# Inverse behind the retention masks, merged softmax steps, a last half row in quarters, memory keys from 512-column products

## Chip, cores and metric

The kernel runs on one core of a Trainium2 chip. The metric is the device time of one execution in microseconds (us), lower is better. The compute engines are TensorE (PE in the rows; PEld is its weight load), VectorE (DVE), ScalarE (ACT) and GpSimd (POOL); SyncE (SP) issues most of the DMAs. Sums of matrix products land in PSUM, which is handed out here in banks of 512 fp32 columns.

## What is computed

A decoder trunk of two layers on 256 tokens of width 1024, with 256 memory tokens. Layer 0 mixes with RWKV-7 heads and retention heads side by side, layer 1 with differential attention; each layer then has a cross attention into the memory and a squared-ReLU MLP. The parts of the reference that matter here:

```python
# retention, by chunks of 128: scores under a decay mask (dmat is zero above the diagonal)
scores = einsum('bhncd,bhnmd->bhncm', qc, kc) * dmat
# RWKV-7: a recurrence over the tokens; the kernel solves it by chunks, with the inverse of a triangular matrix
state = state * w_t + (state @ a_t) * b_t + v_t * k_t
# differential attention, for each of 8 heads
p = softmax(logits)                       # two maps for each head
attn = p[:, :, 0] - lam * p[:, :, 1]
o = rms_norm(attn @ v, ln_w) * (1.0 - lam_init)
# cross attention: keys and values of the normed memory
mem_n = rms_norm(mem, mem_norm_w)
k, v = split(mem_n @ w_kv, 2)
# MLP and the end
h = h + square(relu(norm(h) @ w1)) @ w2
return rms_norm(h, final_norm_w)
```

## The kernel before

**Numbers.** Every large product is made in three products of fp32r operands: each operand is split into a high part (a rounded copy, by ScalarE) and a low part (the difference, by VectorE); `split` at line 128 writes both. A product is high x high, high x low and low x high, summed in PSUM (`mm3_w`, `mm3_x`). A weight piece of 128 x 1024 is loaded by SyncE and split by `wpiece` (line 138): one ScalarE instruction and one VectorE instruction for each of 262 pieces.

**Order.** The program is written stage by stage, but the order on each engine is made by a planner that takes, by priority and by its own model of the times, what is ready. An engine then runs its list strictly in that order. `urgent()` gives a very high priority, `high_priority()` (weight pieces) a high one, and `behind(a, b, ...)` adds an edge that only keeps the order of two instructions. Work without a near consumer, as the keys and values of the memory, fills TensorE where the chains of the RWKV part wait.

**Retention and inverse** (lines 578 to 666). The retention scores of four pairs of heads are small fp32 products into two banks shared by both halves `hq` (`ps1`) and further banks; VectorE multiplies them by the mask (lines 655, 657), ScalarE copies the rest (656). Then `inverse()` solves the triangular system by elimination: a loop of 31 steps of two dependent small VectorE operations (lines 595, 597), whose result `whole_inverse` uses later. All of it is independent of the masks.

**Memory keys** (`kv_chunk`, line 344). For each layer, eight blocks of 128 key columns, two by two in one bank: `proj_cols` runs 8 x 3 matmuls of 256 columns a block, and one ScalarE copy (layer 0, line 349) or one split (layer 1) takes both blocks out. Layer 1's four pairs are spread over the program: `kv1(1)` stands behind the output projection, behind the cross attention of layer 0, ahead of the differential attention, and behind it. `proj_wide` (line 312) is the form that the MLP's up projection uses: for each of 8 parts one matmul of 512 columns over the high and the low part of the activations, which lie side by side (`both`), and one of 256 columns with the low weights; the two halves of the bank are then added (lines 1036, 1037: a ScalarE copy `ul` and a VectorE sum).

**Differential attention** (`diff`, line 1087). The rows are normed, then transposed by TensorE (`turn(0)`, `turn(1)`) in the middle of the memory keys' blocks: behind block 0, and in the middle of block 1. `heads(hd)` makes the scores of a head for two row tiles `t` and two maps `c`, adds the bias, takes the maximum, the exponential with its sum, and then for each `t` a reciprocal (1133), a copy (1134), a factor (1136) and the weighted sum of the maps (1137). `turn_heads` transposes the result. `attend` needs the reciprocals again, squared (1180, 1181).

**End** (`mlp` with `on_sum`, `summed` at line 1218). Of the last of 16 chunks, the four half rows (t, hf) are finished one after the other: six matmuls of 512 columns, the sum into `h` (1063), then `summed`: ScalarE's square with its sum (1226), a step of the mean on VectorE (1232, 1234), GpSimd's power (1236); behind the last half row both tiles are scaled by ScalarE (left half) and VectorE (right half) and stored by SyncE (1244 to 1248).

## Time and profile before

| | us |
|---|---|
| median of 3 runs | 881.5 |
| lowest and highest | 880.51, 882.11 |
| the profiled execution, whole | 881.89 |
| its span, first to last instruction | 880.1 |

| engine | busy us | share |
|---|---|---|
| TensorE | 859.7 | 98% |
| VectorE | 590.4 | 67% |
| ScalarE | 455.2 | 52% |
| GpSimd | 30.8 | 3% |

The table is read from the top: an engine that is busy nearly all the time sets the span, except where it is held up. The ends of matmuls are modelled, and successive ones overlap, so the distance from one start to the next tells more of their cost than their length. Where an engine stood idle ahead of an instruction, the rows give the time in brackets with what released it.

### The profile page before, as it was taken

Reading aid. Unit: us, or ns where it says so; the run is one execution under the profiler, and the core shown is the slowest. Engines: PE = TensorE matmul, PEld = TensorE weight load, DVE = VectorE, ACT = ScalarE, POOL = GpSimd, SP = SyncE. Lnnn points to the kernel's source line nnn. Section 1 sums busy time; section 2 is a strip of 40 time slices with the busy share of each in tenths; the row PEclk is TensorE's granted clock in tenths of the full one; section 3 lists DMA queues with packets and bytes.
Section 4 is the critical chain, followed back from the end, with each engine's and each line's share of the span. In section 5 each row is a group of like instructions: output and inputs, shape, how many; then the busy total and the mean of one; then the engine's idle time right before and its main releaser. Section 6 shows DMA issues by size and latency. Waiting matters only on the chain.

```text
span 880.1 us, 14110 instructions
## 1 busy us (share of the span) xinstructions
PE 859.7 (98%) x5546; PEld 742.7 (84%) x5546; DVE 590.4 (67%) x935; ACT 455.2 (52%) x730; POOL 30.8 (3%) x51
## 2 busy tenths in 40 slices
PE   7999999999999999999999999999999999999996
PEld 5998789888899888888888898878998888888885
DVE  5679888574585576666666668776875766666665
ACT  5775444254564454444444546655655554444443
POOL 3000001010000000000000000000000000000001
PEclk9999999999999999999999999999999999999999
DMA  9754433135654646556555554434542466655551
GB/s 324 238 149 136 140 120 121 51 119 191 221 192 152 206 169 213 192 192 191 190 188 190 175 193 144 144 120 148 192 164 96 158 199 192 191 189 189 187 191 60
DMA packets 47078, 149.98 MB, mean 170 GB/s; under 512 B 4731, under 2 KB 4900, under 8 KB 46884
## 3 DMA queue, kind: packets, MB, share of 16 engines
q1 hardware_dynamic: 45456, 142.73, 50.0%
q10 hardware_dynamic: 1108, 3.72, 1.1%
q0 software_dynamic: 448, 2.63, 0.9%
q8 instruction: 43, 0.70, 0.3%
q14 instruction: 23, 0.19, 0.1%
HBM read 148.01 MB, written 2.63 MB: 171 GB/s over the span
## 4 chain that ended last, share of the span: by engine, by line
PE 90%; DVE 4%; ACT 2%; issue 2%; POOL 1%; DMA 1%; POOLq 0%; SPq 0%; DVEq 0%; ACTq 0%
PE acc L121 38%; PE mm L121 36%; PE tr L121 13%; DVE lo L129 1%; ACT hi L129 1%; PE tr L258 1%; DMA h<-in_x_dram 1%; PE tr L985 1%; PE acc L258 1%; POOL rs L230 0%; DVE xn L272 0%; ACT z L1130 0%; PE tr L1145 0%; PE tr L504 0%; POOL xn L1229 0%
## 5 line engine op out<-in xcount | busy, mean ns | idle before, releaser
L129 DVE TENSOR_TENSOR lo<-raw,hi 128x1024 fp32r<-128x1024 f32 x262 | 320.1, 1224 | 212.7 <-ACT hi L129 210.7
L129 ACT ACTIVATE hi<-raw 128x1024 fp32r<-128x1024 f32 x262 | 277.5, 1060 | 320.2 <-PE mm L121 111.5
L121 PE MATMUL mm<-xhl,hi 128*128 128x256 f32 (+1 forms) x784 | 189.1, 320 | 0.9 <-ACT xhl L129 0.7
L121 PEld LDWEIGHTS mm<-xhl,hi 128*128 128x128 f32 x784 | 129.4, 189 | 13.2 <-issue 2.0
L121 PE MATMUL mm<-xhl,lo 128*128 128x256 f32 x512 | 137.9, 282 | 0.0
L121 PE MATMUL acc<-hi,hl 128*128 128x512 f32 x256 | 100.2, 391 | 0.0
L121 PE MATMUL acc<-hi,hh 128*128 128x512 f32 x256 | 100.1, 391 | 0.0
L121 PE MATMUL acc<-lo,hh 128*128 128x512 f32 x256 | 99.7, 389 | 0.0
L121 PEld LDWEIGHTS mm<-xhl,lo 128*128 128x128 f32 x512 | 96.6, 189 | 2.5
L121 PE MATMUL tr<-xhl,hi 128*128 128x512 f32 x256 | 92.8, 395 | 0.0
L121 PE MATMUL acc<-hi,xhl 128*128 128x512 f32 x256 | 81.9, 396 | 0.0
L121 PE MATMUL tr<-xhl,lo 128*128 128x256 f32 x256 | 66.6, 281 | 0.0
L121 PEld LDWEIGHTS acc<-hi,hl 128*128 128x128 f32 x256 | 48.0, 188 | 11.2 <-DVE hl L129 0.9
L121 PEld LDWEIGHTS acc<-lo,hh 128*128 128x128 f32 x256 | 48.1, 188 | 10.5
L121 PEld LDWEIGHTS acc<-hi,xhl 128*128 128x128 f32 x256 | 47.7, 188 | 9.7
L121 PEld LDWEIGHTS acc<-hi,hh 128*128 128x128 f32 x256 | 48.1, 188 | 8.8
L121 PEld LDWEIGHTS tr<-xhl,hi 128*128 128x128 f32 x256 | 48.2, 188 | 8.5
L121 PEld LDWEIGHTS tr<-xhl,lo 128*128 128x128 f32 x256 | 48.2, 188 | 2.9
L121 PE MATMUL acc<-lo,xhl 128*128 128x512 f32 x128 | 50.4, 393 | 0.0
L121 PE MATMUL mm<-memh,hi 128*128 128x256 f32 x128 | 37.1, 290 | 0.0
L121 PE MATMUL mm<-meml,hi 128*128 128x256 f32 x128 | 37.1, 290 | 0.0
L121 PE MATMUL mm<-memh,lo 128*128 128x256 f32 x128 | 36.6, 286 | 0.0
(320 smaller groups left out, 1342.4 us busy)
## 6 DMA issues: line engine op xcount, KB each, us to landing
raw<-in_w_dram SPq DMA_DIRECT2D x64, 512.0 KB, 4.4
raw<-in_mlp_w_dram SPq DMA_DIRECT2D x64, 512.0 KB, 4.3
raw<-in_hyb_w_in_dram SPq DMA_DIRECT2D x16, 512.0 KB, 3.7
raw<-in_w_k_dram SPq DMA_DIRECT2D x16, 512.0 KB, 3.5
raw<-in_xattn_w_kv_dram SPq DMA_DIRECT2D x16, 512.0 KB, 3.8
raw<-in_w_q_dram SPq DMA_DIRECT2D x16, 512.0 KB, 4.1
raw<-in_xattn_w_o_dram SPq DMA_DIRECT2D x16, 512.0 KB, 3.5
raw<-in_w_dqk_dram SPq DMA_DIRECT2D x16, 512.0 KB, 3.5
```

Of the source, the lines that this page charges most:

```text
L121: ins = nc.tensor.matmul(o, lhsT=lhsT, rhs=rhs, start=start, stop=stop)
L129: return nc.scalar.activation(hi, src, AF.Copy), nc.vector.tensor_tensor(lo, src, r32(hi), op=ALU.subtract)
L258: nc.tensor.transpose(ps[:, k4, :], x[:, kt * 128:(kt + 1) * 128], ident)
L985: nc.tensor.transpose(pt[:, j, m, :], P[:, j, m * 128:(m + 1) * 128], ident)
```

## The change

Four edits that touch different stages.

1. `inverse()`: the first step of the elimination (k = 31) is ordered behind the last mask product of the retention scores.
2. Memory keys: the memory's high and low parts lie side by side in one tile; each block is made by `proj_wide` in a bank of its own and taken out by a ScalarE copy `ul` (one buffer) and a VectorE sum, in layer 1 followed by a split of the block. The turns of the rows in `diff` now stand behind block 0 and behind block 1.
3. `heads`: reciprocal and factor once for both row tiles; the copy goes, `attend` reads the reciprocals in place and multiplies twice. Score tiles have two buffers instead of three.
4. The last half row: its sum over all chunks but the last is added to `h` ahead of the last chunk's products; the last chunk's part is made in two quarters of 256 columns, each in a bank of its own. The second quarter's square is made by VectorE. The left halves of the result are stored from ScalarE's queue.

```diff
     def kv_chunk(layer, i, KT, V, between={}):
 
         if i < 4:
-            def ev(ps):
+            for b in range(2):
+                k = 2 * i + b
+                ps = mm_t().rearrange("p (x t) -> p x t", x=2)
+                proj_wide(I["w_k"][layer], k, memT, ps)
+                ul = kv1pool.tile([128, 256], F32, tag="ul", name=nm("ul"), bufs=1)
+                nc.scalar.activation(ul, ps[:, 1, :], AF.Copy)
                 if layer == 0:
-                    nc.scalar.activation(KT[:, 2 * i:2 * i + 2, :], ps, AF.Copy)
+                    nc.vector.tensor_tensor(KT[:, k, :], ps[:, 0, :], ul, op=ALU.add)
                 else:
-                    split(KT[0][:, 2 * i:2 * i + 2, :], KT[1][:, 2 * i:2 * i + 2, :], ps)
-            proj_cols(I["w_k"][layer], 2 * i, memT, ev, between=between)
+                    nc.vector.tensor_tensor(ul, ps[:, 0, :], ul, op=ALU.add)
+                    split(KT[0][:, k, :], KT[1][:, k, :], ul)
+                if b in between:
+                    between[b]()
...
-            nc.vector.tensor_tensor(pd[:, 0:k, 0:n], Lc[:, k, 0:k].unsqueeze(2).broadcast_to([128, k, n]),
-                                    Xc[:, k:k + 1, m0:16].broadcast_to([128, k, n]), op=ALU.mult)
+            ins = nc.vector.tensor_tensor(pd[:, 0:k, 0:n], Lc[:, k, 0:k].unsqueeze(2).broadcast_to([128, k, n]),
+                                          Xc[:, k:k + 1, m0:16].broadcast_to([128, k, n]), op=ALU.mult)
+            if k == 31:
+                behind(ins, last_mask[0], "the scores' masks first")
...
-                nc.vector.tensor_tensor(d1, ps1[h2][:, hq], cmb, op=ALU.mult)
+                last_mask[0] = nc.vector.tensor_tensor(d1, ps1[h2][:, hq], cmb, op=ALU.mult)
...
+        def last_quarters():
+
+            hh, hl = hts[NCH - 1]
+            ts = slice(128, 256)
+            for c0 in (0, 256):
+                cs = slice(512 + c0, 768 + c0)
+                ps = mm_t()[:, :256]
+                for j in range(2):
+                    wh, wl = wps[NCH - 1][j]
+                    mm3_x(ps, hh[:, j, ts], hl[:, j, ts], wh[:, 0, cs], wl[:, 0, cs], j == 0, j == 1)
+                res(1, 1, c0, c0 + 256, ps)
+                on_sum(1, 2 + c0 // 256)
...
+        if on_sum:
+            res(1, 1)
         for t in range(2):
             for hf in range(2):
+                if on_sum and t == 1 and hf == 1:
+                    last_quarters()
+                    continue
...
-        before({(0, 7): turn(0), (1, 3): turn(1)})
+        before({0: turn(0), 1: turn(1)})
...
+            sm = small.tile([128, 2, 2], F32, tag="sm4", name=nm("sm"))
             for t in range(2):
...
+                mx = small.tile([128, 2], F32, tag="mx2", name=nm("mx"))
+                nc.vector.tensor_reduce(mx, zt[t], axis=AX.X, op=ALU.max, negate=True)
+                for c in range(2):
+                    nc.scalar.activation(zt[t][:, c, :], zt[t][:, c, :], AF.Exp, bias=mx[:, c:c + 1], accum_out=sm[:, t, c:c + 1])
+
+            nc.vector.reciprocal(rsum[:, hd], sm)
+            cf = small.tile([128, 2], F32, tag="cf", name=nm("cf"))
+            nc.vector.scalar_tensor_tensor(cf, sm[:, :, 0], nlam, rsum[:, hd, :, 1], op0=ALU.mult, op1=ALU.mult)
+            for t in range(2):
                 z3 = zt[t]
...
+                nc.vector.scalar_tensor_tensor(z3[:, 0, :], z3[:, 1, :], cf[:, t:t + 1], z3[:, 0, :], op0=ALU.mult, op1=ALU.add)
...
+        if part == 3:
+            nc.vector.scalar_tensor_tensor(fin["sq"][:, 1024:1280], h[:, t, sl], 1.0, h[:, t, sl], op0=ALU.mult,
+                                           op1=ALU.mult, accum_out=ss[:, 3:4])
+        else:
+            nc.scalar.activation(fin["sq"][:, :sl.stop - sl.start], h[:, t, sl], AF.Square, accum_out=ss[:, part:part + 1])
...
-            nc.sync.dma_start(out=out[0, t * 128:(t + 1) * 128, c0], in_=o[:, c0])
+            nc.scalar.dma_start(out=out[0, t * 128:(t + 1) * 128, c0], in_=o[:, c0])
```

## Rows read from the trace of the kernel before

**Rows 1.** The page's part 1: busy us (share of span) and count of each engine.

```profile
PE 859.7 (98%) x5546; PEld 742.7 (84%) x5546; DVE 590.4 (67%) x935; ACT 455.2 (52%) x730; POOL 30.8 (3%) x51
```

**Rows 2.** Order of time, TensorE at 107 us: start, us, engine, line, operation [idle before].

```profile
107.47 1.03 PE L121 MATMUL acc<-qkT,qkT 64*128 64x256 f32 x6
...
110.42 0.83 PE L121 MATMUL tr<-qkT,qkT 64*128 64x128 f32 x6 [1.92 <-DVE PT L657]
```

**Rows 3.** The same stretch, ScalarE and VectorE.

```profile
106.22 1.06 ACT L129 ACTIVATE hi<-raw 128x1024 fp32r<-128x1024 f32 x1 [0.84 <-PE acc L121]
106.25 0.23 DVE L595 TENSOR_TENSOR pd<-Lc,Xc 128x31 f32<-128x31 f32 x1
...
108.14 1.22 DVE L129 TENSOR_TENSOR lo<-raw,hi 128x1024 fp32r<-128x1024 f32 x1
109.28 0.75 DVE L655 TENSOR_TENSOR PT<-mm,prm 128x256 f32<-128x256 f32 x2
```

**Rows 4.** Stretches: us; busy of PE, PEld, DVE, ACT, POOL; granted clock, DMA share, GB/s.

```profile
112.00:114.00 2.00, 2.00 (x7) 1.53 (x8) 1.86 (x8) 0.39 (x1) 0.00 (x0) 0.63 0.09 33
114.00:116.00 2.00, 2.00 (x6) 1.63 (x5) 1.79 (x7) 0.00 (x0) 0.00 (x0) 0.52 0.00 0
...
130.00:150.00 20.00, 19.50 (x179) 18.80 (x182) 17.49 (x46) 10.39 (x18) 3.32 (x2) 1.00 0.35 122
510.00:520.00 10.00, 9.68 (x75) 8.96 (x76) 7.34 (x10) 4.35 (x6) 0.00 (x0) 1.00 0.70 235
```

**Rows 5.** Order of time, TensorE, first and last of 50 key matmuls.

```profile
130.11 0.28 PE L121 MATMUL mm<-meml,hi 128*128 128x256 f32 x1
...
135.99 0.29 PE L121 MATMUL mm<-memh,lo 128*128 128x256 f32 x1
```

**Rows 6.** Chain of waits, one up-projection block of layer 0: start, us, what.

```profile
343.50 2.81 PE mm L121 x16
```

**Rows 7.** Groups by line, form kept apart: count, busy us, mean ns, idle before.

```profile
L1037 DVE TENSOR_TENSOR rl<-tr,ul 128x256 f32<-128x256 f32 x32 | 13.4, 419 | 0.0
...
L1036 ACT ACTIVATE ul<-tr 128x256 f32<-128x256 f32 x32 | 11.7, 366 | 0.0
```

**Rows 8.** Groups by line, the softmax's small operations and its transposes.

```profile
L1145 PE MATMUL tr<-prm,z 128*128 128x128 f32 x24 | 5.3, 283 | 2.1 <-ACT PTd L1146 1.0 <-DVE z L1137 0.6 <-DVE r L1134 0.4
...
L1136 DVE TENSOR_SCALAR cf<-sm,rc,nlam 128x1 f32<-128x1 f32 x16 | 4.3, 266 | 0.0
...
L1134 DVE COPY r<-rc 128x1 f32<-128x1 f32 x16 | 2.4, 147 | 0.1
```

**Rows 9.** Order of time, TensorE, start of the differential attention.

```profile
510.15 1.32 PE L258 MATMUL acc<-prm,xn 128*128 128x128 f32 x8 [0.76 <-DVE xn L272]
...
515.85 0.97 PE L121 MATMUL mm<-xhl,hi 128*128 128x256 f32 x6 [0.17 <-DVE xhl L129]
```

**Rows 10.** Order of time, the end of the program, all engines.

```profile
873.12 0.75 DVE L1063 SCALAR_TENSOR_TENSOR h<-acc,r,h 128x512 f32<-128x512 f32 x1 [0.54 <-PE acc L121]
...
873.17 1.27 POOL L1229 TENSOR_TENSOR xn<-h,row 128x512 f32<-128x512 f32 x1
...
873.85 1.14 DVE L1246 SCALAR_TENSOR_TENSOR xn<-h,rs,row 128x512 f32<-128x512 f32 x1
...
874.50 0.18 ACT L1226 ACTIVATION_READ_ACCUMULATOR fsq<-h 128x1 f32 x1
874.91 0.15 DVE L1234 SCALAR_TENSOR_TENSOR s<-ss,s 128x1 f32<-128x1 f32 x1
...
875.72 0.75 DVE L1246 SCALAR_TENSOR_TENSOR xn<-h,rs,row 128x512 f32<-128x512 f32 x1 [0.66 <-POOL rs L1236]
876.47 0.33 SPq L1245 DMA_DIRECT2D out_dram<-xn  x1
876.85 0.43 SPq L1248 DMA_DIRECT2D out_dram<-xn  x1
```

More of the change, by code (lines that the diff above doesn't have):

```diff
@@ L332, in load_mem @@
     def load_mem(pool):
-        mh = pool.tile([128, 8, 256], F32R, tag="memh", name="memh")
-        ml = pool.tile([128, 8, 256], F32R, tag="meml", name="meml")
+        x = pool.tile([128, 8, 2, 256], F32R, tag="mem", name="memhl")
+        p = Pair((x[:, :, 0, :], x[:, :, 1, :]))
+        p.both = x
+        mh, ml = p
         row = load_row(prep.tile([128, D], F32, tag="kk", name="memrow"), I["mem_norm_w"], nc.scalar)
@@ L576 @@
     Xt = [None]
+    last_mask = [None]
     def inverse():
@@ L941, in cross @@
             qT = [xpool.tile([128, 8, 256], F32R, tag=f"xA{x}", name=nm("qT")) for x in "hl"]
-            Vs = [mempool.tile([128, 2, D], F32R, tag=f"mem{x}", name=nm("Vs")) for x in "hl"]
+            Vs = mempool.tile([128, 2, 2, D], F32R, tag="mem", name=nm("Vs"))
+            Vs = [Vs[:, x] for x in range(2)]
         for t in range(2):
@@ L1057, in down, with res @@
                       wh[:, 0, hf * 512:(hf + 1) * 512], wl[:, 0, hf * 512:(hf + 1) * 512],
-                      c == 0 and j == 0, c == NCH - 1 and j == 1)
-        def res(t, hf):
-            sl = h[:, t, hf * 512:(hf + 1) * 512]
+                      c == 0 and j == 0, c == (NCH - 2 if on_sum and t == 1 and hf == 1 else NCH - 1) and j == 1)
+        def res(t, hf, c0=0, c1=512, ps=None):
+            sl = h[:, t, hf * 512 + c0:hf * 512 + c1]
             with urgent():
-                last_res[0] = nc.vector.scalar_tensor_tensor(sl, acc[t][hf], r2[t], sl, op0=ALU.mult, op1=ALU.add)
+                last_res[0] = nc.vector.scalar_tensor_tensor(sl, acc[t][hf] if ps is None else ps, r2[t], sl, op0=ALU.mult, op1=ALU.add)
+        def last_quarters():
[9 more added lines that the diff above has]
+                on_sum(1, 2 + c0 // 256)
         up(0)
@@ L1101, in diff @@
         PT = dp.tile([128, 8, 384], F32, tag="PT", name="PTd")
-        r1 = dp.tile([128, 2, 8], F32, tag="r1", name="r1")
-        r1q = dp.tile([128, 2, 8], F32, tag="r1q", name="r1q")
+        rsum = dp.tile([128, 8, 2, 2], F32, tag="r1", name="rsum")
         zs = {}
         def heads(hd):
-            zt = [dp.tile([128, 2, 128 * (t + 1)], F32, tag=f"z{t}", name=nm("z"), bufs=3) for t in range(2)]
+            zt = [dp.tile([128, 2, 128 * (t + 1)], F32, tag=f"z{t}", name=nm("z"), bufs=2) for t in range(2)]
             zs[hd] = zt
@@ L1122, in heads @@
                                                    biasM[:, hd, (256 - n):256], op0=ALU.mult, op1=ALU.add)
+            sm = small.tile([128, 2, 2], F32, tag="sm4", name=nm("sm"))
             for t in range(2):
-                n = 128 * (t + 1)
-                z3 = zt[t]
-                mx = small.tile([128, 2], F32, tag="mx2", name=nm("mx"))
-                nc.vector.tensor_reduce(mx, z3, axis=AX.X, op=ALU.max, negate=True)
-                sm = small.tile([128, 2], F32, tag="sm2", name=nm("sm"))
-                for c in range(2):
-                    nc.scalar.activation(z3[:, c, :], z3[:, c, :], AF.Exp, bias=mx[:, c:c + 1], accum_out=sm[:, c:c + 1])
-                rc = small.tile([128, 2], F32, tag="rc2", name=nm("rc"))
-                nc.vector.reciprocal(rc, sm)
-                nc.vector.tensor_copy(out=r1[:, t, hd:hd + 1], in_=rc[:, 0:1])
-                cf = small.tile([128, 1], F32, tag="cf", name=nm("cf"))
-                nc.vector.tensor_scalar(cf, sm[:, 0:1], rc[:, 1:2], nlam, op0=ALU.mult, op1=ALU.mult)
-                nc.vector.scalar_tensor_tensor(z3[:, 0, :], z3[:, 1, :], cf, z3[:, 0, :], op0=ALU.mult, op1=ALU.add)
+                mx = small.tile([128, 2], F32, tag="mx2", name=nm("mx"))
[6 more added lines that the diff above has]
+            for t in range(2):
+                z3 = zt[t]
+                nc.vector.scalar_tensor_tensor(z3[:, 0, :], z3[:, 1, :], cf[:, t:t + 1], z3[:, 0, :], op0=ALU.mult, op1=ALU.add)
         def turn_heads(hd):
@@ L1178, in attend @@
             nc.vector.tensor_reduce(s2, sq, axis=AX.X, op=ALU.add)
-            r1h = r1[:, t, 4 * hq:4 * hq + 4]
-            nc.vector.tensor_tensor(r1q[:, t, 4 * hq:4 * hq + 4], r1h, r1h, op=ALU.mult)
-            nc.vector.tensor_tensor(s2, s2, r1q[:, t, 4 * hq:4 * hq + 4], op=ALU.mult)
+            r1 = rsum[:, 4 * hq:4 * hq + 4, t, 0]
+            for _ in range(2):
+                nc.vector.tensor_tensor(s2, s2, r1, op=ALU.mult)
             rs = rstd_of(s2, 128, 4, EPS)
-            nc.vector.tensor_tensor(rs, rs, r1[:, t, 4 * hq:4 * hq + 4], op=ALU.mult)
+            nc.vector.tensor_tensor(rs, rs, r1, op=ALU.mult)
             on = dp.tile([128, 4, 128], F32, tag="on", name=nm("don"), bufs=2)
@@ L1216, in weigh, with summed @@
         fin["w"] = next_row()
-    def summed(t, hf):
-        sl = slice(hf * 512, (hf + 1) * 512)
-        if hf == 0:
-            fin[t] = (scratch(), small.tile([128, 2], F32, tag="ss", name=nm("ss")),
+    def summed(t, part):
+        sl = (slice(0, 512), slice(512, 1024), slice(512, 768), slice(768, 1024))[part]
+        if part == 0:
+            fin[t] = (scratch(), small.tile([128, 4], F32, tag="ss4", name=nm("ss"), bufs=2),
                       small.tile([128, 1], F32, tag="s1", name=nm("s1")))
@@ L1225, in summed @@
             fin["sq"] = xcpool.tile([128, 8, 256], F32, tag="biasM", name="fsq").rearrange("p a b -> p (a b)")
[L1226 to L1227 removed]
+        if part == 3:
[3 more added lines that the diff above has]
+            nc.scalar.activation(fin["sq"][:, :sl.stop - sl.start], h[:, t, sl], AF.Square, accum_out=ss[:, part:part + 1])
+        if part == 0:
             ins = nc.gpsimd.tensor_tensor(o[:, sl], h[:, t, sl], fin["w"][0], op=ALU.mult)
@@ L1233, in summed @@
             return
-        nc.vector.scalar_tensor_tensor(ms, ss[:, 1:2], 1.0 / D, ms, op0=ALU.mult, op1=ALU.add)
+        nc.vector.scalar_tensor_tensor(ms, ss[:, part:part + 1], 1.0 / D, ms, op0=ALU.mult, op1=ALU.add)
+        if part == 2:
+            return
         rs = small.tile([128, 1], F32, tag=f"rsf{t}", name=nm("rs"), bufs=1)
```

4 lines of the change are left out of this document (1 added, 3 removed).

## The prediction, made before the changed kernel ran

> **What bounds the kernel now.** I read the page first, for the shares of the engines: TensorE is busy for 98% of the span, VectorE for 67% [rows 1]. So a microsecond is gained in three ways only: fewer or shorter TensorE instructions, a wait of TensorE removed, or the ends of the span. Then I read TensorE's waits and, around the longest one behind the opening, the order of time. At 108 us TensorE stops for 1.92 us until VectorE's mask product (line 657) is done [rows 2]. VectorE shows why: from 106.25 us it runs steps of the inverse's elimination (line 595, 597), then one weight piece's low part (line 129), and only at 109.28 the masks of lines 655 and 657 [rows 3]. The reader is to see that VectorE is not short of time here, its order is wrong. Third, the stretches behind that wait: the granted clock falls to about half (the lower level, 1.2 GHz) between 112 and 116 us, with TensorE busy throughout, and stands at 1.00 (2.4 GHz) again from 116 us on [rows 4]. Fourth, the end: behind the last matmul a chain of VectorE, ScalarE, VectorE, GpSimd, then two stores one behind the other on one queue [rows 10].
>
> The profiled execution took 881.9 us, 1.8 us more than its span, and 0.4 more than the median of the three runs (881.5). The sum below is made against 881.9.
>
> **Inverse behind the masks.** The first product of the elimination (k = 31) gets an order edge behind the last mask product, so the whole serial loop stands behind the masks on VectorE. Nothing is added. The eight small steps that stood ahead leave; the weight piece's low part (1.14 us until the next instruction starts) likely stays ahead, for it follows its ScalarE half, which ran from 106.22 to 107.28 [rows 3], and the first masks' matmuls end about 107.6 (the next ones are issued from 107.47 [rows 2]). Low part 107.3 to 108.4, masks from 108.4 in place of 109.28: TensorE goes on 0.9 us earlier. Masks ahead of the low part would give 1.7. What of the clock: the slow stretch costs, by its clock, 2.0 x (1 - 0.63) + 2.0 x (1 - 0.52) = 1.7 us [rows 4]. What came ahead of it was the idle 1.92 us with short 64-row products on both sides. About 1.0 us of idling would be left. The shorter idling of 0.76 us at 510 [rows 9] is not followed by a low clock (1.00 from 510 to 520 [rows 4]), the 1.92 us is; 1.0 is nearer to the former, so I take the 1.7 us back whole. Bounds: nothing of it to 1.7. Sum: -2.6 us, between -0.9 and -3.4.
>
> What is queued behind the edge: the inverse starts later relative to TensorE, and its result is needed by whole_inverse. Its cover is the filler that TensorE takes meanwhile, memory keys and, later, memory values, all needed only by the cross attention far behind. I cost this delay at nothing. Were the cover gone, it would cost the two or three microseconds by which the loop starts later against TensorE.
>
> **Memory keys by 512 columns.** Each of the 16 key blocks (8 for each layer) is now 24 matmuls of 256 columns; it becomes 8 of 512 and 8 of 256, with the same columns. The old step is 0.120 us: 49 steps between the 50 matmuls from 130.11 to 135.99 [rows 5], 2.88 a block. The new form is in this trace, in the MLP's up projection: 16 matmuls in 2.81 us [rows 6]. So 0.07 us a block, 0.56 for each layer. The Trainium skill (TensorE: Matmul & The Clock Gate, Back-to-back issue gap) gives an isolated gap of N/2.4 + 2.5 ns: 24 x 109 = 2.62 us against 8 x 216 + 8 x 109 = 2.60, an estimate of 0.02 a block; the trace's step of 120 ns disagrees with it at 256 columns, and by the page all 16 blocks would bring only 0.3 us.
>
> What it adds: a ScalarE copy (0.37 us) and a VectorE sum (0.42) for each block [rows 7], where one ScalarE copy served two blocks; in layer 1 the split is made by block as well. The first layer's blocks run as filler, with plenty of other filler, so I take its 0.56. The second layer's blocks (four pairs) stand in the norm stages, where the time is set by VectorE and ScalarE turning the rows: TensorE waits 0.76 us for the norm at 510 and 0.17 for the last split at 515.85 [rows 9]. There 0.14 a pair is not gained, as TensorE would only wait longer; and VectorE's two added operations (0.84) may come ahead of the chain. The second turn of the rows moves from the middle of a block to its end (half a block, 1.4 us later at most), but it waits for the norm until 510.15 anyway and TensorE would reach the new place at about 510.4: 0 to 0.25 lost, and what was filler behind it lies ahead of it now. I take 0 for layer 1, between -0.5 and +1.6 (four pairs at up to 0.4). Sum: -0.6, between -1.1 and +1.0.
>
> **Fewer small softmax operations.** A head loses two copies (0.15 each), one factor (0.27) [rows 8] and one reciprocal, which I price like a copy: 0.7 us of VectorE, 5.8 for eight heads. Almost all of it lies beside TensorE's projections. What TensorE waits in these transposes is 2.1 us in all, 1.0 of it on VectorE (0.6 and 0.4), 1.0 on a ScalarE copy [rows 8]. Against it, the first row tile's weights now wait for the second tile's exponentials, as one reciprocal serves both; and two buffers for the scores instead of three make a head's scores wait for the transposes two heads back, which stand ahead of them in TensorE's order. Bounds: +0.7 to -1.2; I take -0.4, less than half of the waits on VectorE.
>
> **Last half row in quarters.** Now: sum into h from 873.12 for 0.75, then ScalarE's square, whose sum is read out at 874.50, mean's step on VectorE 874.91, result scaled from 875.72, second store issued at 876.85 [rows 10]. After: 12 matmuls of 256 columns (1.44) for 6 of 512 (1.39, at the 0.231 that the wide block leaves for each: (2.81 - 8 x 0.12) / 8): +0.1. The last sum covers 256 columns: 0.42 for 0.75 (line 1037 has that shape [rows 7]). The square goes to VectorE: 0.42, without a hop, for the 1.04 from 873.87 (where the sum ends) to 874.91. That makes the mean ready 0.85 us earlier. But GpSimd runs the second tile's product from 873.17 for 1.27 us [rows 10], so its power can't start before 874.44. From the mean's end (874.91 + 0.15) to the scaling at 875.72 power and hops take 0.66 now; from 874.44 that gives 875.0 to 875.1: 0.7 earlier. No row shows VectorE writing a sum of its own: bounds 0 (as the sum of two tensors) to 0.18 more (as ScalarE's read-out at 874.50). The Trainium skill (VectorE: DVE Perf Modes, Two Vector instructions with no wait between them) calls an operation that writes out its accumulator two instructions; by that the upper bound holds, and the wait for GpSimd covers it. The stores go out on two queues, so the second isn't 0.38 behind the first (876.47, 876.85); both still move 256 KB at once, so I take 0.2 of it. The sum of the half row before the last chunk (0.75 on VectorE) is hidden under TensorE's last 24 matmuls. ScalarE's own store holds it for 0.35, with the quarter's square perhaps behind. If the first tile's scaling (1.14 us at 873.85 [rows 10]) comes ahead of the square on VectorE, most is lost. Sum: -0.9, between -0.2 and -1.3.
>
> **Sum.** 2.6 + 0.6 + 0.4 + 0.9 = 4.5: 881.9 - 4.5 = 877.4 us. Best ends together: 3.4 + 1.1 + 1.2 + 1.3 = 7.0, 874.9. Worst ends: 0.9 - 1.0 - 0.7 + 0.2 = -0.6, 882.5.
>
> **Rivals.**
> 1. The masks come first and every wait shrinks (chance 0.18): 1.7 + 1.7 at the masks, 1.1, 0.9, 1.1: 875.5 to 875.0. For it: the matmuls of the masks end about when the low part becomes ready.
> 2. The wait only moves (0.22): the masks gain 0.9, but the clock falls elsewhere or still, the keys' gain is eaten in the norm stages, the end gains 0.5: 881.9 - 1.4 to -2.0 = 880.2. For it: the order of all engines is made anew by the planner, and small waits (0.2 to 0.5 us) may come up anywhere.
> 3. Slower (0.08): the keys' evacuation. VectorE is busy 17.5 of 20 us between 130 and 150 [rows 4], just where the first layer's keys run, and now each block's bank is free only behind ScalarE's copy and VectorE's sum. Two banks: the next but one block needs it 2.81 us later. Behind one weight piece's halves the release takes 1.06 + 0.37 + 1.14 + 0.42 = 3.0, 0.2 too long [rows 3, 7]; behind one more low part 4.1, 1.3 too long. At 1.3 for eight blocks: +10.4 us, 877.4 + 0.6 + 10.4 = 888.4. It makes the kernel slower by over 0.2% from 0.7 us a block on: (883.3 - 878.0) / 8. Against it: between two steps of the elimination other work is slipped in ([rows 3] has a weight piece between steps of it), so a sum rarely waits for more than one weight piece.
> 4. It doesn't do what it says: the elimination was not what held the masks, and they stay at 109.3. Then 2.6 go: 880.0; within rival 2's chance.
>
> **How the numbers follow.** Forecast 877.4 with 0.52 (876 to 879.5). Within 0.2% of 881.5 (879.7 to 883.3, about what a measurement can tell from no change) lie rival 2 and 4; below it the forecast and rival 1, and a little is taken off for ends that add up badly. Faster 0.71, same 0.21, slower 0.08. The range runs from rival 1 (874.9) to the worst end short of the slow rival (881.6).
>
> **What would show it.** Right: no wait of TensorE on line 657 above 1.1 us and a granted clock of 1.0 from 100 to 131 us; keys at 2.81 a block; GpSimd's last power starting within 0.1 us of the end of its product; both last stores issued within 0.1 us. Wrong: a wait of key matmuls on VectorE's sum between 130 and 180 us; longer waits at the norm before the differential attention; a low clock elsewhere; TensorE waiting in the score transposes above 2.1 us.

## The result, and the profile after

| | kernel before | changed kernel |
|---|---|---|
| median | 881.2 us (4 runs, 880.51 to 882.11) | 887.62 us (4 runs, 887.36 to 888.15) |
| ratio | | 1.0057, 95% interval 1.0035 to 1.0079 |
| profiled execution, its span | 881.9, 880.1 us | 887.5, 885.7 us |

The forecast was 877.4 us, faster. The kernel became 6.4 us slower, outside the range (881.6 at most). Of the rivals the third, at 888.4 us, names the mechanism that the runs bear out; it had a chance of 0.08.

The page's part 1 of the changed kernel, which answers to [rows 1], shows nothing of it at first sight. TensorE has 122 instructions fewer and the same busy time, part of it at the lower clock (below); what grew is its idle time.

```profile
PE 860.1 (97%) x5424; PEld 734.1 (83%) x5424; DVE 594.3 (67%) x928; ACT 458.5 (52%) x746; POOL 30.0 (3%) x51
```

**Masks.** In the order of time TensorE now waits 1.08 us for the last mask where [rows 2] had 1.92, and the granted clock of the two stretches behind it is 1.00 where [rows 4] had 0.63 and 0.52. Both as forecast.

```profile
109.86 0.83 PE L121 MATMUL tr<-qkT,qkT 64*128 64x128 f32 x6 [1.08 <-DVE PT L669]
```

```profile
112.00:114.00 2.00, 2.00 (x10) 1.59 (x10) 1.76 (x9) 0.00 (x0) 0.00 (x0) 1.00 0.07 23
114.00:116.00 2.00, 2.00 (x10) 1.62 (x9) 1.79 (x8) 1.06 (x1) 0.00 (x0) 1.00 0.00 0
```

**From 125 to 200 us** that lead is lost. This is TensorE's list of waits there (engine, line, what it waited for: us in total, times, longest), 3.1 us in all. The kernel before has 0.3, 0.3 and 0.2 us in the same stretch.

```profile
PE tr L707 <- DVE xn L700: 0.9, 1, 0.9
PE tr L121 <- DVE xhl L133: 0.6, 1, 0.6
PE acc L121 <- DVE Xn L622: 0.6, 1, 0.6
PE mm L121 <- DVE KT L356: 0.4, 1, 0.4
PE tr L121 <- DVE SCk L583: 0.3, 1, 0.3
PE acc L121 <- DVE U L816: 0.3, 1, 0.3
```

**A pair of the second layer's key blocks** (order of time). The pair's second block begins at 253.9 us, but the first block's copy (line 354) starts at 255.41 and its sum (line 358) at 257.42, behind two weight pieces' low parts (line 129, 2.35 us). The query product, which follows the pair and takes the bank of its first block, starts at 257.89, when that sum has ended; the last key product had been issued at 256.53. The profile names another VectorE instruction as releaser (line 245), the last that ended. e7 below shows that it isn't that one: there the product starts ahead of it.

```profile
255.15 2.35 DVE L129 TENSOR_TENSOR lo<-raw,hi 128x1024 fp32r<-128x1024 f32 x2
...
255.41 0.38 ACT L354 ACTIVATE ul<-mm 128x256 f32<-128x256 f32 x1
...
256.53 0.40 PE L121 MATMUL mm<-memhl,hi 128*128 128x512 f32 x1
...
257.42 0.42 DVE L358 TENSOR_TENSOR ul<-mm,ul 128x256 f32<-128x256 f32 x1
...
257.89 0.39 PE L121 MATMUL mm<-xhl,hi 128*128 128x256 f32 x1 [0.96 <-DVE s L245]
```

In the kernel before, the same query product follows the pair at 257.01 without a wait, although VectorE's half of the pair's split, which reads the pair's bank, comes only at 260.39. A pair held one of the two banks (`ps_mm` has two buffers), and the other was free; now a pair holds both.

```profile
257.01 0.28 PE L121 MATMUL mm<-xhl,hi 128*128 128x256 f32 x1
...
260.39 0.68 DVE L129 TENSOR_TENSOR KT1l<-mm,KT1h 128x512 fp32r<-128x512 f32 x1
```

**The start of the differential attention**, which answers to [rows 9]. TensorE no longer waits for the norm (0.76 us before): the turn stands behind all key products (at 511.67) and finds its rows ready. But nothing is left to do behind it. TensorE waits 1.65 and 1.12 us until ScalarE and VectorE have split the second row tile, and ScalarE's split (513.73) stands behind a weight piece and behind the keys' own split. Then the granted clock is 0.57 from 515 to 523 us (for most of it the lower level, 1.2 GHz). By the clock this stretch costs 8.0 x (1 - 0.57) = 3.4 us (somewhat less, as TensorE waits in a part of it), more than half of the 5.6 by which the span of this execution grew. It isn't lost in every kernel with these waits: e4 has them too, at 1.00.

```profile
511.67 1.04 PE L258 MATMUL acc<-prm,xn 128*128 128x128 f32 x8
...
512.39 1.06 ACT L129 ACTIVATE hi<-raw 128x1024 fp32r<-128x1024 f32 x1 [1.85 <-PE acc L258]
...
513.40 0.42 ACT L129 ACTIVATE KT1h<-ul 128x256 fp32r<-128x256 f32 x1
513.73 1.07 ACT L129 ACTIVATE xhl<-acc 128x512 fp32r<-128x512 f32 x2
...
514.36 0.38 PE L121 MATMUL mm<-xhl,hi 128*128 128x256 f32 x1 [1.65 <-ACT xhl L129]
...
516.68 0.58 PE L121 MATMUL mm<-xhl,hi 128*128 128x256 f32 x1 [1.12 <-DVE xhl L129]
```

```profile
515.00:523.00 8.00, 6.88 (x35) 6.68 (x35) 4.12 (x7) 1.86 (x3) 0.00 (x0) 0.57 0.42 148
```

**The end**, which answers to [rows 10]. The first tile's scaling (line 1282) starts at 878.09 beside GpSimd's product and takes 1.74 us; the last quarter's square (line 1257) waits for it until 879.82. From the last sum to the last scaling it is 881.10 - 877.55 = 3.55 us, where [rows 10] have 875.72 - 873.12 = 2.60.

```profile
877.55 0.48 DVE L1076 SCALAR_TENSOR_TENSOR h<-mm,r,h 128x256 f32<-128x256 f32 x1
...
878.01 1.26 POOL L1263 TENSOR_TENSOR xn<-h,row 128x512 f32<-128x512 f32 x1
...
878.09 1.74 DVE L1282 SCALAR_TENSOR_TENSOR xn<-h,rs,row 128x512 f32<-128x512 f32 x1
...
879.82 0.41 DVE L1257 SCALAR_TENSOR_TENSOR fsq<-h 128x256 f32<-128x256 f32 x1
...
880.16 0.07 DVE L1257 DVE_READ_ACCUMULATOR fsq<-h 128x1 f32 x1
...
881.10 0.75 DVE L1282 SCALAR_TENSOR_TENSOR xn<-h,rs,row 128x512 f32<-128x512 f32 x1 [0.67 <-POOL rs L1272]
```

**A loss that no wait shows.** In the chain of waits a chunk's down projection (24 products of 512 columns) in the first layer takes 5.51 us in the changed kernel, 5.45 in the kernel before. The edits don't touch it. The 15 chunks of each MLP lose about 1.4 us together: 11.14 us instead of 11.08 from chunk to chunk in the first layer, 11.12 instead of 11.09 in the second.

```profile
360.57 5.51 PE acc L121 x24
```

```profile
360.21 5.45 PE acc L121 x24
```

### The profile page after: what moved, and what is told of

Its sections match the earlier page's. It is cut to its first block, busy times and chain, and to the rows that moved or that the text cites. A ratio compares the mean times of both kernels' runs of the same rounds, so it can differ in the third digit from the quotient of the medians.

```text
span 885.7 us, 13883 instructions
## 1 busy us (share of the span) xinstructions
PE 860.1 (97%) x5424; PEld 734.1 (83%) x5424; DVE 594.3 (67%) x928; ACT 458.5 (52%) x746; POOL 30.0 (3%) x51
## 4 chain that ended last, share of the span: by engine, by line
PE 87%; DVE 6%; ACT 2%; issue 2%; POOL 1%; DMA 1%; POOLq 0%; SPq 0%; DVEq 0%; ACTq 0%
PE acc L121 38%; PE mm L121 34%; PE tr L121 12%; DVE lo L129 2%; ACT hi L129 1%; DVE xn L272 1%; DMA h<-in_x_dram 1%; POOL rs L230 1%; PE tr L998 1%; PE tr L258 0%; ACT z L1159 0%; PE tr L1174 0%; DVE xhl L129 0%; PE tr L513 0%; POOL xn L1263 0%
## 5 line engine op out<-in xcount | busy, mean ns | idle before, releaser
L121 PEld LDWEIGHTS acc<-lo,hh 128*128 128x128 f32 x254 | 47.7, 188 | 10.4
L121 PE MATMUL mm<-memhl,hi 128*128 128x512 f32 x128 | 47.0, 401 | 0.4 <-DVE KT L356 0.4
L121 PE MATMUL mm<-hi,memhl 128*128 128x512 f32 x128 | 40.9, 397 | 0.0
L121 PE MATMUL mm<-memhl,lo 128*128 128x256 f32 x128 | 35.2, 294 | 0.0
```

The source lines that it names most:

```text
L121: ins = nc.tensor.matmul(o, lhsT=lhsT, rhs=rhs, start=start, stop=stop)
```

## The experiments

My theory after the comparison: the memory keys cost it all, by their sum on VectorE. The rivals: the inverse's delay ate the lead between 131 and 190 us; the tail; something else. The first four kernels do one part of the change alone. (The two score buffers instead of three go with every kernel but e1, as room is short; e9 tells what they cost.) The kernel before was timed beside each set: 881.43, 881.44, 881.0 and 881.53 us.

**e1: masks alone.**

```
+            if k == 31:
+                behind(ins, last_mask[0], "the scores' masks first")
...
-                nc.vector.tensor_tensor(d1, ps1[h2][:, hq], cmb, op=ALU.mult)
+                last_mask[0] = nc.vector.tensor_tensor(d1, ps1[h2][:, hq], cmb, op=ALU.mult)
```

> Kernel before with only the order edge (elimination behind the masks). Theory 1 (the keys' new form ate the lead of the masks): VectorE starts the elimination some 6 us later, the fillers cover it, no low clock at 112 to 116 us, and the lead of about 2 us of 126 us is still there at 190 us: 879.2 us (878.2 to 880.0), 2.0 below the kernel before. Theory 2 (the inverse's delay has no cover and is what ate the lead between 131 and 190 us): TensorE waits 1 us for the transposed rows at 133 us, the lead at 190 us is 0.3 or less: 880.9 to 882.

880.77 us against 881.43, ratio 0.9985 (0.9969 to 1.0). The wait for the last mask is 1.08 us, the clock 1.00, and TensorE's list of waits from 125 to 200 us shows 0.5 and 0.3 us and none for the inverse: theory 2 falls for this part alone. But the gain is a third of what I expected. The clock accounts for part of that, see e14: the kernel before doesn't lose its 1.7 us in every execution.

**e2: softmax alone** (the hunks of `heads` and of `r1`).

```
-                nc.vector.tensor_copy(out=r1[:, t, hd:hd + 1], in_=rc[:, 0:1])
...
+            nc.vector.reciprocal(rsum[:, hd], sm)
+            nc.vector.scalar_tensor_tensor(cf, sm[:, :, 0], nlam, rsum[:, hd, :, 1], op0=ALU.mult, op1=ALU.mult)
```

> Kernel before with only the merged softmax operations (two score buffers for three). The prediction took 0.4 us for them. Theory 1: the differential attention of the changed kernel gained 2.8 us on the kernel before, between 536 and 589 us, by these operations: 878.6 us (878.2 to 879.2). Theory 2: it only won back what the disturbed norm stage ahead of it (503 to 523 us) had lost, and without that stage the gain is the predicted one: 880.8 (880.4 to 881.2).

881.57 us, ratio 1.001 (0.9991 to 1.0029): neither theory's reason. The differential attention was shorter in the trace, and all of it was lost again in the two MLPs, where no edit is. The chain of waits has the down projection at 5.58 us for 5.45:

```profile
357.77 5.58 PE acc L121 x24
```

**e3: tail alone** (the hunks of `down`, `res`, `last_quarters`, `summed`).

```
+        if part == 3:
+            nc.vector.scalar_tensor_tensor(fin["sq"][:, 1024:1280], h[:, t, sl], 1.0, h[:, t, sl], op0=ALU.mult,
+                                           op1=ALU.mult, accum_out=ss[:, 3:4])
```

> Kernel before with only the last half row in quarters and the ScalarE store queue (the score buffers are two instead of three, only to make room). Theory 1: the first tile's scaling stands ahead of the square on VectorE and costs more than the shorter sum gives: about 1.1 us slower, 882.3 (881.8 to 882.8); the last scaling starts 5.5 us or more behind the last matmul of the kernel where it was 3.1 in the kernel before. Theory 2 (the prediction): the scaling fits in ahead, or is covered by GpSimd's product: 880.3.

885.08 us, ratio 1.004 (1.0017 to 1.0064): more than either theory. From the last sum (876.19) to the last scaling (879.74) it is 3.55 us, 0.95 more than before, as theory 1 had it. The rest is again in the MLPs: 5.59 us for each down projection.

**e4: memory keys alone** (the hunks of `load_mem`, `kv_chunk`, `Vs` and the turns).

```
+                proj_wide(I["w_k"][layer], k, memT, ps)
...
+                nc.scalar.activation(ul, ps[:, 1, :], AF.Copy)
...
+                    nc.vector.tensor_tensor(ul, ps[:, 0, :], ul, op=ALU.add)
```

> Kernel before with only the memory keys by 512 columns, their sum and split by block, the one memory tile and the moved second turn of the rows (score buffers two instead of three to make room). Theory 1 (these cost it all): 5 to 10 us slower, 887 to 891, with a half clock behind the norm stage at 510 us, and 1.5 to 2 us lost between 130 and 190 us, about 5 between 503 and 523, 1.6 between 629 and 642. Theory 2 (the inverse's delay shares in it): between 130 and 190 us nothing is lost, and the sum is 3 to 6 us. The prediction: 880.6.

889.3 us, ratio 1.0097 (1.0059 to 1.0136). The waits of the changed kernel are all there: 0.8, 0.6, 0.4 and 0.3 us between 125 and 200 us, 1.0 us at 259, 1.7 and 1.1 us at 516 and 518, 0.5 and 0.6 us at 638 and 644. The keys are the loss; which of their four edits is open. Its size is not known well: the four runs go from 887.38 us (mean granted clock 0.994) to 894.11 (0.987), and the interval from 5.2 to 12 us.

**e5: the lie of the tiles.** In the compiled programs, e2 and e3 have one thing in common: their new small tiles push the tiles of the rows and of the MLP's hidden activations up, by 128 and 64 bytes; in the whole change it is 192. So e5 is the kernel before with an idle tile. The traces hold no addresses; what bears these distances out is that idle tiles which complete them to 256 bytes (128 in e9 and e13, 192 in e10, 64 in e12 and e16) bring the chunks of the first layer back to 11.08 us.

```
     const.tile([128, 16], F32, name="pad")
+    small.tile([128, 16], F32, tag="pads", name="pads", bufs=1)
```

> Kernel before with nothing but one unused 64-byte tile in the pool of small tiles (and two score buffers instead of three, to make room), which moves the MLP's and the rows' tiles by 64 bytes, as the tail's new sum tiles do. Theory 1 (where these tiles lie sets the step of the wide matmuls): an MLP chunk takes 11.21 us in both layers instead of 11.08 and 11.09, as in the kernel with the tail alone, and the whole is 2.5 to 3.5 us slower: 884.4. Theory 2 (the chunk's period is set by something else that the tail and softmax edits do): 11.08 and 11.09, and 881.4.

884.78 us against 881.44, ratio 1.0022 (1.0002 to 1.0042). The chunks take 11.21 and 11.22 us, those of e3 to the hundredth, and the down projection 5.59. Theory 1 holds: 64 idle bytes cost 2 to 3 us (0.22% by the ratio, 3.3 by the medians).

```profile
359.24 5.59 PE acc L121 x24
```

**e6: the second turn back in mid-block.**

```
+            if kt == 3 and mid:
+                mid()
...
-        before({0: turn(0), 1: turn(1)})
+        before({0: turn(0), (1, 3): turn(1)})
```

> Memory keys alone (as in e4) with the second turn of the rows back in the middle of the second block instead of at its end. Theory 1 (the turn moved past the key matmuls that hid the second row tile's split): the waits behind that turn, 1.9 and 1.3 us at 513 to 518 us in e4, fall to some 1.5 together as in the kernel before, and the time falls by 1.6 or more: 887 (885.8 to 887.6 where e4 had 889.3 in the median and 887.4 at best). Theory 2 (the added copy, sum and splits of each block come ahead of the rows' split on VectorE and ScalarE): the waits only change place, 888 to 889.5.

887.68 us, 1.6 less than e4 in the median. By the times alone that isn't shown: e4's two best runs (887.38, 887.57) are as short as those of e6 (887.27 at best). TensorE's order of time has 0.88 and 0.34 us in place of 1.66 and 1.11, the pattern of [rows 9]. Theory 1 holds for the waits at this place. The other waits of e4 stay.

```profile
516.52 1.32 PE L258 MATMUL acc<-prm,xn 128*128 128x128 f32 x8 [0.88 <-DVE xn L272]
...
519.58 0.39 PE L121 MATMUL mm<-xhl,hi 128*128 128x256 f32 x1 [0.34 <-ACT xhl L129]
```

**e7: copy and sum urgent.**

```
+                with urgent():
+                    nc.scalar.activation(ul, ps[:, 1, :], AF.Copy)
...
+                        nc.vector.tensor_tensor(ul, ps[:, 0, :], ul, op=ALU.add)
```

> Memory keys alone (as in e4) with the copy and the sum of each block marked urgent, so that the planner puts them ahead of the weights' low parts. Theory 1 (a pair of blocks now holds both banks, and the next product waits for the first block's sum, which stands behind weight pieces): the waits of 1.1 us at 259, 0.7 at 638 and 0.7 at 644 us vanish or fall below 0.3, and the time falls by 2 to 2.5: 886 to 887. Theory 2 (those waits are for the rows' factors, not for the bank): they stay, 888 to 890.

882.56 us, ratio 1.0003 (0.9984 to 1.0022): 6.7 less than e4, more than theory 1 had asked for. The sum that stood at 257.42 now stands ahead of the two low parts, and the query product (254.67) doesn't wait; it starts before the instruction of line 245 (256.00), so what had held it was the bank. The list of waits is empty from 240 to 262 us, and from 125 to 200 too, where I had counted on nothing.

```profile
253.06 0.42 DVE L359 TENSOR_TENSOR ul<-mm,ul 128x256 f32<-128x256 f32 x1
...
253.39 2.35 DVE L129 TENSOR_TENSOR lo<-raw,hi 128x1024 fp32r<-128x1024 f32 x2
...
254.67 0.28 PE L121 MATMUL mm<-xhl,hi 128*128 128x256 f32 x1
...
255.66 0.42 DVE L129 TENSOR_TENSOR KT1l<-ul,KT1h 128x256 fp32r<-128x256 f32 x1
...
256.00 0.21 DVE L245 TENSOR_SCALAR s<-ss 128x1 f32<-128x1 f32 x2
```

**e8: wide keys in the first layer only.**

```
+            if layer == 1:
+                proj_cols(I["w_k"][layer], 2 * i, memT,
+                          lambda ps: split(KT[0][:, 2 * i:2 * i + 2, :], KT[1][:, 2 * i:2 * i + 2, :], ps), between=between)
+                return
```

> Memory keys by 512 columns in the first layer only; the second layer's keys, its split by pairs and the turns are as in the kernel before. Theory 1 (the first layer's sums hold VectorE, and TensorE, up between 131 and 190 us): 2 to 3 us are lost there and nothing later: 883.9 (883.0 to 884.6). Theory 2 (the prediction): 0.5 us gained, 880.9. Theory 3 (all the cost is in the second layer's norm stages): 881.4.

884.17 us, ratio 1.003 (1.0009 to 1.0052): 2.7 us lost; in the trace it lies before 200 us: from TensorE's first product of `rkv` with the masked scores `PT` to its first transpose of `yc` it is 197.29 - 128.39 = 68.90 us, 190.81 - 124.63 = 66.18 before. So of e4's 7.9 the second layer has 5.1 by the medians. The waits that e4's trace lists there, less those of the kernel before, are 3.9 us, 1.8 of it behind the turn.

**e9: softmax, the tiles put back.** e2 with an idle tile of 128 bytes, so that all tiles lie as in the kernel before, modulo 256 bytes.

```
+    small.tile([128, 32], F32, tag="pads", name="pads", bufs=1)
```

> The merged softmax operations alone (as in e2) with an unused tile of 128 bytes beside their new small tile, so that the rows' and the MLP's tiles lie as in the kernel before, modulo 256 bytes. Theory 1 (e2 gained 2.5 to 3 us in the differential attention and lost as much by the lie of the tiles): MLP chunks of 11.08 and 11.09 us, 878.6 us (878.0 to 879.4). Theory 2 (the gain in the differential attention is only made up of delays ahead of it): 880.8 to 881.4.

879.41 us against 881.0, ratio 0.9988 (0.9977 to 0.9999); the chunks are at 11.08 and 11.09. Theory 1 holds, at the upper end of its range. From the first product behind the turn to the first transposes of the next norm it is 625.18 - 518.29 = 106.89 us in e9, 624.91 - 515.85 = 109.06 before ([rows 9] for 515.85): 2.2 us. First e9, then the kernel before:

```profile
518.29 0.98 PE L121 MATMUL mm<-xhl,hi 128*128 128x256 f32 x6 [0.17 <-DVE xhl L129]
...
625.18 0.60 PE L258 MATMUL tr<-prm,xn 128*128 128x128 f32 x4
```

```profile
584.52 0.33 PE L1145 MATMUL tr<-prm,z 128*128 128x128 f32 x1 [1.03 <-ACT PTd L1146]
...
624.91 0.60 PE L258 MATMUL tr<-prm,xn 128*128 128x128 f32 x4
```

The groups by line (count, busy us, mean ns, idle before) have 0.4 us of idling before the score transposes in e9 for the 2.1 of [rows 8]. The 1.03 us at 584.52, the last heads' transposes waiting for a copy of ScalarE, is gone with the rest; of the 2.2 us, 1.7 are such waits; where the rest comes from stays open. Two score buffers cost nothing: with them and the old softmax, e10 has 624.07 - 515.02 = 109.05 us for the 109.06.

```profile
L1144 PE MATMUL tr<-prm,z 128*128 128x128 f32 x24 | 4.8, 283 | 0.4
```

**e10: the tail with two order edges** and an idle tile of 192 bytes.

```
-            behind(ins, last_res[0], "the sums of the last tile first")
+            behind(ins, fin["mean"], "the mean of the last tile first")
...
+            behind(ins, fin["last sq"], "the squares first")
```

> The tail's quarters alone (as in e3), laid as in the kernel before by an unused tile of 192 bytes, and with two order edges: ScalarE's scaling of the first tile behind the last of its squares, VectorE's scaling of the first tile behind the last mean. Theory 1 (that scaling, 1.75 us beside GpSimd's product, held the square up): from the start of the last sum to the start of the last scaling 2.5 us (2.60 in the kernel before, 3.55 in e3), MLP chunks of 11.08 and 11.09, 881.1 (880.6 to 881.6). Theory 2 (the chain is long for another reason): 3.2 us or more from sum to scaling, 882.3.

882.62 us against 881.0, ratio 1.0027 (1.0013 to 1.0041). Theory 1 falls: 875.72 - 872.37 = 3.35 us from sum to scaling. The square now starts at once, 0.08 us behind GpSimd's product, and takes 1.46 us; in the changed kernel it took 0.41 with GpSimd idle. Whichever of the two VectorE instructions stands there is held until the product is done.

```profile
872.37 0.48 DVE L1064 SCALAR_TENSOR_TENSOR h<-mm,r,h 128x256 f32<-128x256 f32 x1 [0.17 <-PE mm L121]
...
872.80 1.27 POOL L1253 TENSOR_TENSOR xn<-h,row 128x512 f32<-128x512 f32 x1
...
872.88 1.46 DVE L1247 SCALAR_TENSOR_TENSOR fsq<-h 128x256 f32<-128x256 f32 x1
...
875.72 0.75 DVE L1273 SCALAR_TENSOR_TENSOR xn<-h,rs,row 128x512 f32<-128x512 f32 x1 [0.44 <-POOL rs L1262]
```

**e11: the keys with both remedies** (e6 and e7 together).

> The memory keys alone with both remedies: copy and sum urgent (e7), second turn in the middle of the second block (e6). Theory: with no bank wait and the turn's cover back, what is left is the saving of the wide products, 0.07 us for each of 16 blocks, and the waits of 509 to 513 us fall from 3.2 in e7 to 1.8 or less: 880.9 (880.2 to 881.5). Rival: the added VectorE and ScalarE work still delays the rows' split, 882 and more.

878.97 us against 881.0, ratio 0.9977 (0.9961 to 0.9992): 10 us below e4, and below the kernel before. The waits at 507 and 511 us are 0.87 and 0.60. The gain is larger than the 1.1 us of the wide products: from 125 to 200 us the list of waits, 0.8 us in all in the kernel before, is empty.

**e12: the whole change, mended** (e6, e7, e10 and an idle tile of 64 bytes).

> The whole change with its three mishaps mended: copy and sum of the keys urgent, second turn in the middle of the block, the tail's two order edges, and an unused tile of 64 bytes that puts the rows' and the MLP's tiles back to the lie of the kernel before. Theory: masks 0.9, softmax 2.8, keys 0.5, tail 0.3 gained: 877.0 (876.0 to 878.5), below both kernels. Rival: the parts undo each other's gains in the differential attention or between 131 and 190 us, 879.5 and more.

879.26 us against 881.0, ratio 0.9982 (0.9974 to 0.9991): below both kernels, 2 us above my number and next to the rival's. The parts don't add up: TensorE waits for the inverse at 157 us, which it doesn't in e11 (see e14), and the tail still costs.

**e13 and e14: softmax and mended keys, without and with the masks' edge**; no tail, tiles put back by 128 bytes.

> Softmax and memory keys with both remedies and the tiles' lie of the kernel before (an unused tile of 128 bytes); masks and tail as in the kernel before. Theory: the gains of e9 (1.6) and e11 (2.0) add up, as they lie in different stages: 877.4 (876.6 to 878.4). Rival: they overlap, 878.5 to 879.5.

> As e13, with the order edge of the masks. Theory 1 (the edge gains 0.84 us at the masks and gives it back where the inverse's result is waited for, near 156 us): within 0.5 us of e13, and a wait of 0.6 to 1.0 us of the first products with the inverse. Theory 2 (the delay is covered, as the prediction had it): 0.8 us or more below e13.

e13: 877.95 us against 881.53, ratio 0.9962 (0.9949 to 0.9976), the fastest kernel of the study; its gains are those of e9 and e11 added. e14: 878.45 us, 0.9962 (0.9948 to 0.9975). Theory 1 holds, by the waits: the half microsecond between the two medians is less than the spread of either kernel's runs. In TensorE's order of time, e13 first, the wait for the last mask is 1.89 and 1.08 us; e14 has another wait of 0.56 us for the inverse (0.83 with the step into the small products), e13 none.

```profile
111.00 0.83 PE L121 MATMUL tr<-qkT,qkT 64*128 64x128 f32 x6 [1.89 <-DVE PT L671]
```

```profile
111.19 0.83 PE L121 MATMUL tr<-qkT,qkT 64*128 64x128 f32 x6 [1.08 <-DVE PT L674]
...
157.12 1.07 PE L121 MATMUL acc<-Xn,SCb 32*32 32x32 f32 x56 [0.56 <-DVE Xn L627]
```

The granted clock from 108 to 124 us (the windows' last column but two) is 0.89 in e13, 1.00 in e14, and 1.00 in e2, which has the long wait too (2.05 us). In all, the six profiles with the edge (changed kernel, e1, e12, e14, e15, e16) have 1.00. Of the twelve without, seven have 0.79 to 0.89 (before, e3, e5, e6, e8, e9, e13) and five 1.00 (e2, e4, e7, e10, e11). First e13, then e2:

```profile
108.00:124.00 16.00, 14.11 (x65) 11.22 (x62) 13.70 (x42) 5.28 (x9) 0.00 (x0) 0.89 0.30 111
```

```profile
108.00:124.00 16.00, 13.95 (x73) 11.38 (x69) 15.14 (x44) 6.90 (x10) 0.00 (x0) 1.00 0.37 130
```

**e15 and e16: the whole change with one remedy each**, copy and sum urgent in e15, an idle tile of 64 bytes in e16.

> The whole change with one remedy: copy and sum of the keys urgent. Theory (the wait for the keys' bank is the largest part of the loss): 6 to 7 us below the changed kernel, 881 (880 to 882), the waits of about 1 us at 133, 0.6 at 138, 1.1 at 256, 0.7 at 635 and 642 us gone; what stays is the turn's place, the tail and the tiles' lie. Rival: 2 to 3 us below, 885, the loss lying in the sum of many small delays.

> The whole change with nothing but an unused tile of 64 bytes, which puts the rows' and the MLP's tiles back, modulo 256 bytes, to where the kernel before has them. Theory: MLP chunks of 11.08 and 11.09 us instead of 11.14 and 11.12, 15 in each layer: 1.4 us, and the time 886.2 (885.4 to 887.0). Rival: other stages lose what the MLP gains, 887.6.

e15: 881.82 us, ratio to the kernel before 0.9993 (0.997 to 1.0016). By the medians that one remedy takes back 5.8 of the 6.4 us. Part of this is the clock: the changed kernel's four runs have a mean granted clock of 0.990 and 0.991, e15's ten go from 0.987 to 0.995, and the two at 0.990 take 882.8 and 883.68 us, 4 to 5 less than the changed kernel. At 510 and 512 us 1.6 and 1.2 us of waiting stay (the turn). e16: 886.27 us, 1.0063 (1.0048 to 1.0078); the down projection is at 5.45 again and 1.35 us are back, as the chunks have it; that the medians of four runs each (885.3 to 887.72 in e16) agree with them so closely is luck. Both theories hold, e15's 5.8 just under its 6 to 7.

## Why the prediction was wrong, point by point

**Masks: -2.6.** The wait shrank by 0.84 us, forecast 0.9. The clock's 1.7 us, taken back whole, was mis-sized: with the wait of 1.9 to 2.05 us the clock falls in some executions and not in others (7 of 12 profiles), so the one profile that I had read gave the price of the drop, not its chance. The masks alone brought 0.7 us, with an interval down to none.

**"I cost this delay at nothing."** This step failed in the whole change. The cover, the filler, holds in e1; with the keys in their new form it runs dry and TensorE waits for the inverse, 0.6 us in the changed kernel's list, 0.83 in e14: as much as the masks gain. The price that the prediction gave for a lost cover, two or three microseconds, was too high.

**Memory keys: -0.6, between -1.1 and +1.0.** This is the term that turned the sign: +7.9 us alone (e4). The size of the block was right. Five pairs of products, one of 512 and one of 256 columns, take 510.97 - 509.22 = 1.75 us in the order of time of the changed kernel, so a block of eight takes 2.80, forecast 2.81.

```profile
509.22 0.39 PE L121 MATMUL mm<-memhl,hi 128*128 128x512 f32 x1
...
510.97 0.40 PE L121 MATMUL mm<-memhl,hi 128*128 128x512 f32 x1
```

What failed is what stands behind it. First, "a sum rarely waits for more than one weight piece", the argument against rival 3: the sum of 257.42 waits for two, and nothing had told the planner that a bank hangs on it. The old form had one bank for a pair, emptied by one ScalarE copy in the first layer and by a split in the second, and left the other bank free; the new one holds both banks until VectorE comes round. Whether the second bank or the added step on VectorE weighs more, no run tells apart. Rival 3 had this chain with its price. I gave it 0.08 because it needed more than one piece, and I had put it between 130 and 180 us alone. e8 has 2.7 us there, not 10.4; the greater part, 5.1 by the medians, lies in the norm stages, where I had allowed 1.6. That the rival's 888.4 came so near is luck. Second, the turn's move: "0 to 0.25 lost" looked at when the turn's rows are ready, and not at what it left uncovered. The half block behind the old place hid the split of the second row tile. Without it TensorE waits 2.8 us there (e4) instead of 1.2 (e6), and the clock may fall behind the wait: in three of the five profiles with the turn at the end (changed kernel, e7, e16), in none of the thirteen with it in mid-block. In the medians, each against the kernel before timed beside it, the turn's place is worth 1.6 us (e4, e6) and 3.2 (e7, e11).

**Softmax: -0.4, between +0.7 and -1.2.** Right sign, outside the bounds: 2.2 us in the stage, 1.6 in the median (e9, interval 0.1 to 2.0). I had counted waits on VectorE alone. The 1.0 us on a ScalarE copy belonged to the same chain, for at the last heads nothing else is left to do and the whole chain is in the open. In the changed kernel the gain was there and was lost to the lie of the tiles.

**Tail: -0.9, between -0.2 and -1.3.** The sentence that the first tile's scaling might come ahead of the square came true, but "most is lost" was too mild: 0.95 us from sum to scaling are added. The order is not the cause (e10). The step that failed is the price of the square, 0.42 us: beside GpSimd's product it takes 1.46. [Rows 10] had shown it, and I had read past it: the same scaling takes 1.14 us at 873.85, beside that product, and 0.75 at 875.72. The Trainium skill has the rule (SBUF — State Buffer, Who interferes with whom): a VectorE instruction with two SBUF inputs contends with a GpSimd instruction that reads SBUF, for ports under an exclusive lock, and the order of issue decides which of them waits. The traces agree: the square ends 0.27 us behind the product in e10, the scaling 0.56 in the changed kernel, and the sum at 873.12 in [rows 10], which has one input in PSUM, isn't stretched. As in the prediction, the accumulator's read-out is an instruction of its own, 0.07 us. The two queues for the stores, forecast at 0.2, gained nothing: the last two are issued together (881.85 and 881.88), as forecast, but from the start of the last scaling to the end of the span it is 885.7 - 881.1 = 4.6 us, 880.1 - 875.7 = 4.4 before.

**The signs that I had named.** Of those for wrong, three came: a key product waiting for VectorE's sum (line 356, 0.4 us), longer waits before the differential attention (2.8 us in all for 0.9), and a low clock elsewhere (0.57 from 515 to 523 us). GpSimd's last power starts at 880.51, 1.2 us behind the end of its product and not within 0.1.

**Not in the sum at all:** the lie of the tiles, +1.35 us in the whole change (e16), more in its parts (e2, e3).

The sum from the runs for the whole change: keys 7.9, lie of the tiles 1.35, tail some 1, softmax -1.6, masks -0.7, together 8.0; measured 6.4. The difference says nothing, as the keys' 7.9 alone are known to 5.2 to 12 us. In the one traced execution of the changed kernel the low clock behind the turn is the largest single loss, 3.4 us by the clock. It stands behind the turn, which edit 2 moved.

## What to carry to other kernels

Before a product is spread over more banks, count the banks that stay free, and find the instruction that empties each bank, what is queued ahead of it on its engine, and who takes the bank next; where the planner can't see the urgency, say it. When a step is moved behind filler, ask what that filler hid behind the old place. Test each part of a change alone, beside an idle tile of the same size: here gains of up to 2 us stood beside losses of 8, 1.4 and 1 us, and the lie of the tiles masked the gain of one part.

## What the runs showed that I had not expected

The step of a product depends on where its operands lie. With the rows' and hidden activations' tiles 0, 64, 128 and 192 bytes (modulo 256) from their place in the kernel before, the 24 products of a down projection in the first layer take 5.45, 5.59, 5.58 and 5.51 us (before, e5, e2, changed kernel). The up projection's blocks stay at 2.79 to 2.82 throughout. In the down projection the moved tiles are the stationary operand and the weights, which didn't move, the streamed one; in the up projection it is the other way round. That points to the load of the stationary operand, but the two operands were not moved apart.

A VectorE instruction of 0.41 us became one of 1.46 us beside a GpSimd product of 1.27 us (e10).

Behind the same wait the granted clock fell in some executions and not in others: from 508 to 528 us it is 1.00 in e4, which waits 1.7 and 1.1 us there, and 0.83 in the changed kernel, which waits as long. What decides it stays open. The medians carry this chance with them, and differences of 1 to 2 us between kernels timed in a few runs are to be read with it.
